# Earlier filler weights, a seventh key tile and later layer-two tables in a two-layer attention kernel

## The chip, the cores and the metric

The kernel runs on one NeuronCore of a Trainium2 chip. The metric is the device time of one execution in microseconds (us). Two executions of this kernel are told apart when they differ by more than about 0.2%, some 5 us.

## The reference

Two transformer layers over 2048 tokens of width 1024, in float32. Layer one projects x into queries, keys and values of six stick-breaking heads, six differential heads and four memory heads, and into gates; layer two has sliding-window attention with sinks in place of the first two. Each layer multiplies its mixed heads by silu(gate), applies an output matrix, adds the scaled input and normalises.

```python
log_1mb = where(strict, log_sigmoid(-z), 0);  after = reverse_cumsum(log_1mb) - log_1mb
sb_o    = where(strict, exp(log_sigmoid(z) + after), 0) @ v               # stick-breaking
df_o    = rms_norm((softmax(s[0]) - lam * softmax(s[1])) @ v, g) * 0.8    # differential
mem_o   = softmax(mq @ mk.T / 8) @ mv                                     # memory
y       = concat(sb_o, df_o, mem_o) * silu(gate) @ w_out
x       = layer_norm(sqrt(2) * x + y, g, b)        # sqrt(2) = (2 * DEPTH) ** 0.25
```

Queries and keys of the differential heads and of layer two are rotated (`_partial_rope`) by tables of cosines and sines.

## The kernel before

The program is one long sequence of stages, in each of which TensorE (PE) is given the most to do. Each f32 product of a projection is made of three matmuls on a high and a low part of its operands (hi·hi, hi·lo, lo·hi); `wtile`, `wsplit` and `split` make such parts with a cast on ScalarE (ACT) and a subtraction on GpSimd (POOL) or VectorE (DVE).

- `layer1_proj`, about 0 to 700 us: tiles of 128 output features by four token chunks of 512 (`t`), 24 matmuls each, into three PSUM banks ("mm"). Features 0 and 1 of its middle loop (`k` = 0, 1) are the memory queries. Beside each of their eight chunks `next(tables)` computes one step of the rotation tables: four steps of layer one (`rope1`), then four of layer two (`rope2`). A step is one DMA of positions, some eight DVE instructions, and on ACT an Abs and two Sin. From `k` = 2 a memory unit runs beside each chunk (`next(side)`): scores, softmax, transposes, values. The last part, `gates`, is 32 chunks of sigmoid and multiply.
- `stick_breaking`, about 715 to 1076 us: three pairs of heads `p`, each with four query chunks `t` = 3, 2, 1, 0, four blocks `qi` of 128 queries in each, and key chunks `c` = t to 0. A unit (p, t, qi, c) is scores on PE, two sigmoids on ACT, two scans on DVE, two multiplications on POOL, two groups of transposes on PE with copies on ACT and DVE, and value products on PE. Scores are made three units (`SB_AHEAD`) ahead of the transposes. Here SyncE (SP), PE, DVE and ACT run in the order of the code, and POOL in the order of a scheduler. `begin(p, t)` issues loads when the scores of a chunk begin.
- `differential`, about 1076 to 1616 us: three pairs, each in two halves `k` of four units `j`: scores, exponentials, a mixture of two softmaxes, transposes, values. Beside it `filler` makes part of the output projection from five of its eight weight tiles: it loads raw weights into three "rx" buffers (`wload`), splits them (`wsplit`: ACT cast, POOL subtraction), and works through 32 blocks. Its first steps, the ones before the first `yield`, run inside `stick_breaking`: four in `begin(2, 1)`, and one beside each of the last ten units. PE and ACT run in the order of the code here, the rest in the scheduler's.
- Keys of the differential stage are tiles of 512 keys, named "kc" (three buffers) and "kd" (three). `load_dk` picks the tag from a list by the number of the load; a load into a buffer waits until the tile before it there has been read. Pair 0 is loaded in `begin(2, 1)`. The next pair's chunks 3, 2 and 1 are asked for at the end of a pair's first half and chunk 0 at the end of its second. Values come through four "vc" buffers (`load_dv`).
- `join`, `layer2_kv`, `gates`, `layer2` and a last `out_proj` follow. In `out_proj` each block of 128 rows ends in a layer norm: mean and variance on DVE (`bn_aggr`), plus epsilon and power -0.5 on POOL, and a scaling on DVE.

All DMAs but a few are issued by SP, in one order. A DMA names the semaphores that it waits for, and those behind it wait with it.

Of the kernel before, what the change touches and what calls it, by code (L numbers as in the profile page):

```python
# [8 lines left out]
F32R = mybir.dt.float32r  # L9
# [8 lines left out]
P = 128  # L18
NB = S // P
TC = 512  # L20
NT = S // TC
NEG = -1e30
ALPHA = 4.0 ** 0.25
EPS = 1e-5
# [8 lines left out]
FT = 1  # L33
# [33 lines left out]
class Net:  # L67
# [216 lines left out]
    def layer1_proj(self):  # L284
        nc, dr = self.nc, self.dr
# [33 lines left out]
        for k, dst in enumerate((0, 1, self.sbq[1], self.sbk[1], self.sbq[2], self.sbk[2])):  # L319
            w = nxt  # L320
            for t in range(NT):
                ps = self.proj_t(w, t)
                if k < 2:
                    q = self.t("c2")
                    nc.scalar.mul(q, ps, 0.125)  # L325
                    for hh in range(2):
                        qs = self.t("c2", F32R)
                        self.qstack_head(qs, q, hh, nc.gpsimd)
                        self.dma(self.mq[dst, t, :, hh], qs)
                    next(tables)  # L330
                else:
                    self.spill_parts(ps, dst, t)
                    next(side)
                if t == 1:
                    nxt = self.wtile(W[rows[k + 1]]) if k < 5 else self.vtile(0)
                if t == 2 and k > 1 or t % 2 and k < 2 and k + t < 4:
                    next(kvs)
            if k == 1:
                side = self.memory(*self.mkv)
                kvs = self.memkv(self.i["wmo"], mem, False)  # L340
                next(kvs)
# [11 lines left out]
        for p in range(3):  # L353
            for base, dst in ((9, self.dfq), (12, self.dfk)):
                w = nxt
                for t in range(NT):
                    if t == 2:
# [8 lines left out]
        gates = self.gates(W[20:28], self.silu, self.om, self.m1,  # L366
                           [(f, t) for f in range(6) for t in range(NT)] + [(f, t) for t in range(NT) for f in (6, 7)])
        for k, _ in enumerate(gates):
            if k == 24 + GATES_A:
                qs = self.load_qstack(self.sbq[0], NT - 1)  # L370
                self.sb_first = (*self.load_sb(0), qs)
# [171 lines left out]
    def stick_breaking(self):  # L543
# [9 lines left out]
        def begin(p, t):  # L553
            sls[p, t] = self.load_silu(self.silu[p], t)
            k = chunks.index((p, t)) + 1
            if k < len(chunks):
                qs[chunks[k]] = self.load_qstack(self.sbq[chunks[k][0]], chunks[k][1])
            if t == NT - 2 and p < 2:
                kv[p + 1] = self.load_sb(p + 1)
            if p == 2 and t == FT:  # L560
                self.fill = self.filler()
                steps.extend(next(self.fill))
                for f in steps[:4]:
                    f()
                del steps[:4]
                self.dk, self.dq = {}, {}
                self.load_dq(0, 0, 0)
                for c in range(NT):
                    self.load_dk(0, c)
# [66 lines left out]
        for k, u in enumerate(units):  # L636
            if k + SB_AHEAD < len(units):
                scores(units[k + SB_AHEAD])
            turn(u)
            if k + SB_AHEAD < len(units):  # L640
                weights(units[k + SB_AHEAD])
            if u[0] == 2 and k > len(units) - 11:
                for f in steps[:1]:
                    f()
                del steps[:1]
            while k - done >= SB_GROUP or k == len(units) - 1 and done <= k:
                for v in units[done:done + SB_GROUP]:
                    values(v)
                done += SB_GROUP
        self.nc = nc  # L650

    def differential(self):
# [21 lines left out]
                f()  # L674
            del steps[:k]

        for c in range(NT):
            self.load_dv(0, c)
        for s in range(-2, len(units)):
            scores, new = self.diff_scores(units[s + 2], rows) if s + 2 < len(units) else ([[]] * 4, [])  # L680
# [30 lines left out]
        return [None] * (14 - len(tail)) + tail  # L711

    def load_dk(self, p, c):
        k_ = self.t(("kc", "kc", "kc", "kd", "kd", "kd", "kc", "kc", "kd", "kc", "kd", "kc")[len(self.dk)], F32R, [P, 4, 512])
        for g in range(4):
            self.dma(k_[32 * g:32 * g + 32], self.dfk[p][g // 2, :, c * 512:c * 512 + 512].rearrange("(h r) t -> r h t", h=4))
        self.dk[p, c] = k_
# [22 lines left out]
    def diff_scores(self, unit, rows):  # L740
# [15 lines left out]
        def chunk(hc, w, c):  # L756
            nc = self.nc
            qb, t, qi, n, col = parts[w]
            nch = (n + 511) // 512
            if c == 0 and w == 0:  # L760
                if hc == 0:
                    begin()
                rows[unit][0].append((self.t("row"), self.tiny(8, tag="mn", bufs=8)))
            e, mn = rows[unit][0][hc]
            mn = mn[:, 4 * w:4 * w + 4]
            lo, hi = c * 512, min(n, c * 512 + 512)
            m = hi - lo
            z = self.psum("z")
            diag = hi == n
            q = self.dq[p, k, j // 2, w][:, hc, (qi % 2) * P:(qi % 2 + 1) * P]  # L770
            nc.tensor.matmul(z[:, :m], q, self.dk[p, c][:, hc, :m], start=True, stop=True)
            before = mn[:, :1] if w and c else 3e38
            acc, n0 = mn[:, c:c + 1], max(0, m - 3 * P) if diag else m
            if n0:
                nc.vector.tensor_scalar(e[:, col + lo:col + lo + n0], z[:, :n0], -scale, before, ALU.mult, ALU.min, accum_out=acc)  # L775
            if diag:
                nc.vector.tensor_tensor_reduce(e[:, col + lo + n0:col + hi], z[:, n0:m], self.mask[:, 3 * P + n0 - m:3 * P], -scale,
                                               acc if n0 else before, ALU.add, ALU.min, acc)
            if w and c == 0:
                first, k_ = rows[unit][0][hc][1], (parts[0][3] + 511) // 512  # L780
                nc.vector.tensor_reduce(first[:, :1], first[:, :k_], AX.X, ALU.min)  # L781
            if diag and w and hc == 3 and j == 3 and p < 2:
                for c in ((3, 2, 1) if k == 0 else (0,)):
                    self.load_dk(p + 1, c)

        def exps(hc, w):
# [123 lines left out]
    def filler(self):  # L910
# [7 lines left out]
        def wload(h, k):  # L918
            raws[k] = self.t("rx", F32, [P, 512])
            self.dma(raws[k], i["woute"][tiles[k], :, 512 * h:512 * h + 512])  # L920
# [33 lines left out]
        def finish(f):  # L954
# [1 line left out]
            self.nc.vector.scalar_tensor_tensor(res[f], res[f], ALPHA, res["ps"], ALU.mult, ALU.add)  # L956
            self.dma(self.rp[tb, :, 512 * h:512 * h + 512], res[f])

        yield ([lambda: load(0)] + [lambda k=k: wload(0, k) for k in range(3)]
               + [f for k in range(5) for f in (lambda k=k: wsplit(0, k), *([lambda k=k: wload(0, k + 3)] if k < 2 else []))]  # L960
               + [lambda: split(0), lambda: load(1)])
        for f in range(len(blocks)):
            p = [lambda f=f, c=c: products(f, c) for c in range(5)]
            r, s, l, e = lambda f=f: resid(f), lambda f=f: split(f + 1), lambda f=f: load(f + 2), lambda f=f: finish(f)
# [63 lines left out]
    def out_proj(self, w, msrc, spans, res, alpha, lng, lnb, tbs, ahead):  # L1028
# [20 lines left out]
        for k, tb in enumerate(tbs):  # L1049
# [15 lines left out]
            mvr = self.tiny(2)  # L1065
            nc.vector.bn_aggr(mvr, st.rearrange("p (a s) -> p a s", a=2))
            rs = self.tiny(1)
            nc.gpsimd.tensor_scalar_add(rs, mvr[:, 1:2], EPS)  # L1068
            nc.gpsimd.tensor_tensor(rs, rs, self.mhalf[:, :1], ALU.pow)
            nc.vector.scalar_tensor_tensor(r, r, mvr[:, 0:1], g, ALU.subtract, ALU.mult)  # L1070
            if alpha:
# [344 lines left out]
    def run(self):  # L1416
        nc, dr, i = self.nc, self.dr, self.i
        with self.phase({"c2": 3, "sl": 2}, {}):
# [9 lines left out]
            self.rp = dr.tile([NB, P, D], F32, name="rp")  # L1428
            self.silu2 = [dr.tile([P, S], F32, name=f"silu2_{f}") for f in range(8)]
            self.m2 = dr.tile([8, P, S], F32, name="m2")  # L1430
            with self.phase({"qd": 2, "wT": 7, "vc": 4, "row": 9},
                            {"mm": 1, "z": 3, "tp": 2, "pv": 2}):
                tail = self.differential()
            keys.close()
# [88 lines left out]
```

## Time and profile before

| | |
|---|---|
| time, median of 3 runs | 2544.74 us (2543.16 to 2546.1) |
| the profiled execution | 2546.16 us, its span 2544.40 us |
| TensorE busy | 2392.6 us, 94% |
| VectorE, ScalarE, GpSimd busy | 62%, 49%, 37% |
| mean granted TensorE clock | 0.984 |

The profile is of one execution. The span is the time between its first and its last instruction. Busy time is counted per engine; for TensorE the ends of matmuls are modelled. "Idle before <-X" is the time in which an engine stood still before an instruction, with what released it. The granted clock is a share of 2.4 GHz; half of it is 1.2 GHz.

### The profile page before, as it was taken

Reading aid. Unit: us, or ns where it says so; the run is one execution under the profiler, and the core shown is the slowest. Engines: PE = TensorE matmul, PEld = TensorE weight load, DVE = VectorE, ACT = ScalarE, POOL = GpSimd, SP = SyncE. Lnnn points to the kernel's source line nnn. Section 1 sums busy time; section 2 is a strip of 40 time slices with the busy share of each in tenths; the row PEclk is TensorE's granted clock in tenths of the full one; section 3 lists DMA queues with packets and bytes.
Section 4 is the critical chain, followed back from the end, with each engine's and each line's share of the span. In section 5 each row is a group of like instructions: output and inputs, shape, how many; then the busy total and the mean of one; then the engine's idle time right before and its main releaser. Section 6 shows DMA issues by size and latency. Waiting matters only on the chain. (4 is left out here: it accounts for less than half of the span.)

```text
span 2544.4 us, 42300 instructions
## 1 busy us (share of the span) xinstructions
PE 2392.6 (94%) x15564; PEld 1939.8 (76%) x15564; DVE 1573.6 (62%) x3657; ACT 1254.2 (49%) x2453; POOL 939.3 (37%) x800
## 2 busy tenths in 40 slices
PE   9999999999999999789889888899999999999998
PEld 7778998888877777557667666778788777777887
DVE  5733222431168888699899899684312676777455
ACT  4443222221158777567677677443212777776100
POOL 0401002750057878611111021464612655534333
PEclk9999999999999999899999999999999999999999
DMA  7643222331334431944543341563323655533641
GB/s 280 208 156 131 82 84 79 127 132 56 107 90 111 93 84 34 215 122 109 128 112 94 103 109 46 181 204 109 86 98 112 163 153 154 144 97 101 199 144 64
DMA packets 199247, 311.60 MB, mean 122 GB/s; under 512 B 17920, under 2 KB 97280, under 8 KB 198528
## 3 DMA queue, kind: packets, MB, share of 16 engines
q1 hardware_dynamic: 198464, 307.83, 40.8%
q8 instruction: 124, 2.03, 0.4%
q10 hardware_dynamic: 576, 1.05, 0.1%
q14 instruction: 83, 0.68, 0.1%
HBM read 204.74 MB, written 104.07 MB: 121 GB/s over the span
## 5 line engine op out<-in xcount | busy, mean ns | idle before, releaser
L57 PE MATMUL psmm<-big,w 128*128 128x512 f32 x1680 | 414.9, 395 | 1.3 <-ACT c L325 1.3
L57 PEld LDWEIGHTS psmm<-big,w 128*128 128x128 f32 x1680 | 306.6, 189 | 59.4 <-ACT c L325 1.5
L57 ACT COPY wT<-pstp 128x512 f32<-128x512 f32 (+3 forms) x400 | 203.4, 525 | 188.6 <-PE pstp L57 185.0
L608 POOL TENSOR_TENSOR wb<-wb,row 128x512 f32<-128x512 f32 (+3 forms) x240 | 262.6, 1117 | 72.8 <-DVE row L57 47.5
L57 DVE TENSOR_TENSOR_SCAN row<-s,row,pszero 128x512 f32<-128x512 f32 (+5 forms) x240 | 254.3, 1105 | 51.8 <-ACT s L57 33.4
L254 PE MATMUL psmm<-big,w 128*128 128x512 f32 x1200 | 275.2, 390 | 0.0
L254 PEld LDWEIGHTS psmm<-big,w 128*128 128x128 f32 x1200 | 225.1, 188 | 46.9 <-issue 0.2
L57 PE MATMUL psmm<-big,mp 128*128 128x512 f32 x1056 | 246.6, 394 | 3.4 <-POOL big L1015 3.4
L57 ACT ACTIVATE row<-row,mn 128x2048 f32<-128x2048 f32 (+7 forms) x192 | 229.8, 1202 | 13.9 <-DVE mn L781 10.1
L57 PEld LDWEIGHTS psmm<-big,mp 128*128 128x128 f32 x1056 | 199.7, 190 | 45.3 <-POOL big L1015 3.8
L775 DVE TENSOR_SCALAR_CACHE_REDUCE row<-psz 128x512 f32<-128x512 f32 (+1 forms) x324 | 200.2, 640 | 20.7 <-PE psz L57 19.8
L1234 DVE TENSOR_TENSOR c<-psmm,c 128x512 f32<-128x512 f32 x62 | 42.7, 691 | 240.3 <-ACT c L1233 240.3
L945 POOL TENSOR_TENSOR mp<-mp,mp 128x640 fp32r<-128x640 f32 x32 | 52.0, 1625 | 343.4 <-ACT mp L57 282.7
L57 PE MATMUL pstp<-ident,wb 128*128 128x128 f32 x816 | 118.2, 277 | 35.4 <-DVE wT L57 15.4
L817 DVE SCALAR_TENSOR_TENSOR row<-row,tiny,row 128x128 f32<-128x128 f32 (+7 forms) x144 | 149.4, 1088 | 0.4
L57 PE MATMUL psmm<-wo,mp 128*128 128x512 f32 x480 | 147.7, 420 | 1.4 <-POOL mp L945 0.9
L209 POOL TENSOR_TENSOR w<-w,w 128x1024 fp32r<-128x1024 f32 x20 | 48.8, 2440 | 256.3 <-ACT w L208 107.5
L1233 ACT ACTIVATE c<-psmm 128x512 f32<-128x512 f32 x62 | 36.8, 596 | 212.8 <-PE psmm L254 204.5
L57 PE MATMUL pstp<-ident,row 128*128 128x128 f32 x816 | 130.5, 281 | 6.4 <-ACT wT L57 5.6
L57 PEld LDWEIGHTS pstp<-ident,wb 128*128 128x128 f32 x816 | 92.2, 141 | 56.6 <-POOL wb L608 24.8
L1191 ACT ACTIVATE e<-e,tiny 128x256 f32<-128x256 f32 (+1 forms) x192 | 94.7, 494 | 60.5 <-DVE e L1189 60.1
L57 PEld LDWEIGHTS pstp<-ident,row 128*128 128x128 f32 x816 | 99.6, 143 | 30.8 <-ACT wT L57 13.4
(232 smaller groups left out, 5003.0 us busy)
## 6 DMA issues: line engine op xcount, KB each, us to landing
silu<-c SPq DMA_DIRECT2D x54, 256.0 KB, 2.3
sl<-silu SPq DMA_DIRECT2D x54, 256.0 KB, 3.3
qs<-sbq SPq DMA_DIRECT2D x48, 256.0 KB, 5.3
cs<-rope SPq DMA_DIRECT2D x24, 512.0 KB, 4.6
kc<-k SPq DMA_DIRECT2D x36, 320.0 KB, 5.0
w<-in_we_dram SPq DMA_DIRECT2D x20, 512.0 KB, 3.6
raw<-in_wo_dram SPq DMA_DIRECT2D x20, 512.0 KB, 3.8
rx<-in_x_dram SPq DMA_DIRECT2D x32, 256.0 KB, 2.7
```

The source lines that it names most:

```text
L57: return self.tc.keep_in_program_order(f(*a, **k))
L209: eng.tensor_sub(lo[:, sl], raw[:, sl], hi[:, sl].bitcast(F32))
L254: self.nc.tensor.matmul(ps, w[a][:, c, :], self.xpart(t, c, b), start=(c == k == 0), stop=(c == 7 and k == 2))
L608: nc.gpsimd.tensor_mul(w[:, hh, :m], w[:, hh, :m], prr[:, lo:hi])
L775: nc.vector.tensor_scalar(e[:, col + lo:col + lo + n0], z[:, :n0], -scale, before, ALU.mult, ALU.min, accum_out=acc)
L817: self.nc.vector.scalar_tensor_tensor(x[:, lo:hi], y[:, lo:hi], cf[hh][:, w:w + 1], x[:, lo:hi], ALU.mult, ALU.add)
L945: self.nc.gpsimd.tensor_sub(ml, m, mh.bitcast(F32))
L1191: nc.scalar.activation(e[:, hh, ns:], e[:, hh, ns:], AF.Exp, bias=nmx[:, hh:hh + 1], scale=-1.0, accum_out=s[:, hh:hh + 1])
L1233: nc.scalar.activation(sg, ps, AF.Sigmoid)
L1234: nc.vector.tensor_mul(sg, ps, sg)
```

## The change

- The four `rope2` steps move from the chunks of `k` = 1 to the gates, ahead of chunks 2, 7, 12 and 17.
- The filler's first steps begin in `begin(2, 3)`: three weight loads there, the five splits and the other two loads beside the units of chunk (2, 3) with odd `c`. The loads and the split of the first two mixed blocks run beside chunk (2, 1). The differential stage's first queries and keys are asked for in `begin(2, 2)`.
- A seventh key tile "ke" exists during `differential`; the list of tags is new, and all four chunks of the next pair are asked for at the end of a pair's first half. The first values are loaded in the order 3, 0, 1, 2.
- In `out_proj` epsilon is added on DVE in place of POOL.

```diff
@@ layer1_proj
-                    next(tables)
+                    if k == 0:
+                        next(tables)
...
         for k, _ in enumerate(gates):
+            if k % 5 == 2 and k < 20:
+                next(tables)
@@ stick_breaking, begin
-            if p == 2 and t == FT:
+            if p == 2 and t == NT - 1:
                 self.fill = self.filler()
                 steps.extend(next(self.fill))
-                for f in steps[:4]:
+                for f in steps[:3]:
                     f()
-                del steps[:4]
+                del steps[:3]
+            if p == 2 and t == NT - 2:
                 self.dk, self.dq = {}, {}
@@ stick_breaking, loop over units
-            if u[0] == 2 and k > len(units) - 11:
-                for f in steps[:1]:
-                    f()
-                del steps[:1]
+            if steps and (u[0] == 2 and u[1] == NT - 1 and u[3] % 2 and len(steps) > 3 or u[0] == 2 and u[1] == FT):
+                steps.pop(0)()
@@ differential
-        for c in range(NT):
+        for c in (3, 0, 1, 2):
             self.load_dv(0, c)
@@ load_dk
-        k_ = self.t(("kc", "kc", "kc", "kd", "kd", "kd", "kc", "kc", "kd", "kc", "kd", "kc")[len(self.dk)], F32R, [P, 4, 512])
+        k_ = self.t(("kc", "kc", "kc", "kd", "kd", "kd", "ke", "kd", "kc", "kc", "kc", "kd")[len(self.dk)], F32R, [P, 4, 512])
@@ diff_scores
-            if diag and w and hc == 3 and j == 3 and p < 2:
-                for c in ((3, 2, 1) if k == 0 else (0,)):
+            if diag and w and hc == 3 and j == 3 and k == 0 and p < 2:
+                for c in range(NT - 1, -1, -1):
@@ filler
-        yield ([lambda: load(0)] + [lambda k=k: wload(0, k) for k in range(3)]
+        yield ([lambda k=k: wload(0, k) for k in range(3)]
...
-               + [lambda: split(0), lambda: load(1)])
+               + [lambda: load(0), lambda: load(1), lambda: split(0)])
@@ out_proj
-            nc.gpsimd.tensor_scalar_add(rs, mvr[:, 1:2], EPS)
+            nc.vector.tensor_scalar_add(rs, mvr[:, 1:2], EPS)
@@ run
-            with self.phase({"qd": 2, "wT": 7, "vc": 4, "row": 9},
+            with self.phase({"qd": 2, "wT": 7, "vc": 4, "row": 9, "ke": 1},
```

DVE, first memory unit, before. Lines 181 to 188 are a table step; L486, L491 and L495 are the softmax (maximum, reciprocal, scaling) of the scores `psz`:

```order
L182 TENSOR_SCALAR c_159_1015<-c_159_1015,freq 128x512
L184 TENSOR_SCALAR c_160_1018<-c_159_1015 128x512
L185 TENSOR_SCALAR c_160_1018<-c_160_1018 128x512
L187 SCALAR_TENSOR_TENSOR c_159_1015<-c_160_1018,c_159_1015 128x512
L486 TENSOR_REDUCE tiny_1072<-psz_1066 128x2
L265 TENSOR_TENSOR c_165_1059<-psmm_1033,c_164_1058 128x512
L187 SCALAR_TENSOR_TENSOR c_159_1015<-c_160_1018,c_159_1015 128x512
L491 RECIPROCAL tiny_1077<-tiny_1074 128x2
L187 SCALAR_TENSOR_TENSOR c_159_1015<-c_160_1018,c_159_1015 128x512
L495 TENSOR_SCALAR c_168_1071<-c_168_1071,tiny_1077 128x256 x2
```

The same place in the change (the softmax's lines are three higher):

```order
L469 COPY mv_263<-psmm_872 128x128
L469 COPY mv_263<-psmm_882 128x128
L489 TENSOR_REDUCE tiny_1004<-psz_998 128x2
L265 TENSOR_TENSOR c_153_991<-psmm_965,c_152_990 128x512
L494 RECIPROCAL tiny_1009<-tiny_1006 128x2
L498 TENSOR_SCALAR c_156_1003<-c_156_1003,tiny_1009 128x256 x2
```

No table step stands ahead of the softmax or inside it any more.

SP in the third pair of `stick_breaking`, before. `rx<-in_woute` are raw weights, `qs` the queries and `sl` the gates of a chunk, `m<-c` a chunk's result, `qa`, `kc` and `kd` the first queries and keys of the next stage:

```order
L57 DMA rx_9765<-in_woute_dram 128x512
L57 DMA rx_9767<-in_woute_dram 128x512
L57 DMA rx_9769<-in_woute_dram 128x512
L57 DMA qa_9771<-dfq_241 32x4x256 x4
L57 DMA qa_9776<-dfq_241 32x4x256 x4
L57 DMA kc_9781<-dfk_244 32x4x512 x4
L57 DMA kc_9786<-dfk_244 32x4x512 x4
L57 DMA kc_9791<-dfk_244 32x4x512 x4
L57 DMA kd_9796<-dfk_244 32x4x512 x4
L57 DMA m_255<-c_1761_9941 128x512
L113 DMA kd_11131<-dfk_245 32x4x512 x4
L113 DMA kd_11136<-dfk_245 32x4x512 x4
L57 DMA rx_10055<-in_woute_dram 128x512
```

And in the change, two chunks earlier in the stage:

```order
L57 DMA qs_8766<-sbq_237 64x2x512 x4
L57 DMA rx_8771<-in_woute_dram 128x512
L57 DMA rx_8773<-in_woute_dram 128x512
L57 DMA rx_8775<-in_woute_dram 128x512
L57 DMA m_255<-c_1533_8903 128x512
L57 DMA rx_8966<-in_woute_dram 128x512
L57 DMA rx_9116<-in_woute_dram 128x512
L57 DMA sl_9343<-silu_251 128x512
L113 DMA rx_10382<-in_x_dram 128x512
L57 DMA qs_9345<-sbq_237 64x2x512 x4
L57 DMA qa_9350<-dfq_241 32x4x256 x4
```

Before, the fourth weight load stands behind 24 loads of keys; in the change all five stand ahead of them, and of the queries of chunk (2, 1).

## Rows read from the trace of the kernel before

**Rows 1.** The page's first part: busy us, share of the span and instructions of PE and the other engines.

```profile
PE 2392.6 (94%) x15564; PEld 1939.8 (76%) x15564; DVE 1573.6 (62%) x3657; ACT 1254.2 (49%) x2453; POOL 939.3 (37%) x800
```

**Rows 2.** Stretches of the span: from and to, length, busy us (and instructions) of PE, weight loads, DVE, ACT and POOL, then the granted clock, the DMA share and GB/s.

```profile
100.00:200.00 100.00, 91.23 (x468) 74.37 (x469) 47.87 (x93) 41.99 (x91) 15.38 (x9) 0.95 0.50 162
...
600.00:700.00 100.00, 100.00 (x443) 82.86 (x442) 15.77 (x23) 11.38 (x19) 0.00 (x0) 1.00 0.28 88
...
1000.00:1100.00 100.00, 77.34 (x629) 60.84 (x627) 70.05 (x127) 58.52 (x93) 56.20 (x72) 0.90 0.74 175
```

**Rows 3.** What PE waited for, over the whole span: us in total, times, the longest.

```profile
PE psz L57 <- DVE row L775: 31.9, 51, 2.5
PE pstp L57 <- ACT wT L57: 21.5, 16, 14.1
...
PE psz L57 <- DMA kc<-dfk: 8.4, 2, 6.9
PE pstp L57 <- DVE c L495: 7.8, 1, 7.8
```

**Rows 4.** PE in order of time at the first memory units: start, us, instruction, count, idle time before it. `psz` are scores, `pstp` transposes, `psmm` the 24 matmuls of a projection.

```profile
117.50 0.64 PE L57 MATMUL psz<-w,w 128*128 128x256 f32 x4
...
131.37 1.11 PE L57 MATMUL pstp<-ident,c 128*128 128x128 f32 x4 [7.77 <-DVE c L495]
...
133.13 6.90 PE L57 MATMUL psmm<-big,w 128*128 128x512 f32 x24
...
158.25 0.66 PE L57 MATMUL pstp<-ident,c 128*128 128x128 f32 x4
...
166.34 5.63 PE L57 MATMUL psmm<-big,w 128*128 128x512 f32 x24
```

**Rows 5.** DVE and ACT there, in order of time: the first and the last DVE instruction of a table step, the maximum of the first scores, and ACT's table load ahead of their exponentials.

```profile
116.16 2.64 DVE L181 CAST c<-c 128x512 f32<-128x512 int32 x1 [5.92 <-DMA c<-in_pos_dram]
...
124.33 0.43 DVE L188 TENSOR_SCALAR c<-c 128x512 f32<-128x512 f32 x1
...
127.19 0.68 DVE L486 TENSOR_REDUCE tiny<-psz 128x2 f32<-128x512 f32 x1
...
127.95 1.28 ACT L489 ACT_TABLE_LOAD   x1 [0.78 <-DVE tiny L486]
```

**Rows 6.** SP's issues in the third pair, and one cast and one subtraction of a filler weight on ACT and POOL. The us of an SP row run from its first issue to the end of its last.

```profile
945.06 2.53 SPq L57 DMA_DIRECT2D qs<-sbq  x4
...
983.86 2.53 SPq L57 DMA_DIRECT2D qs<-sbq  x4
...
1018.34 3.59 SPq L57 DMA_DIRECT2D qs<-sbq  x4
...
1024.66 5.80 SPq L57 DMA_DIRECT2D qa<-dfq  x8
...
1048.27 8.82 SPq L113 DMA_DIRECT2D kd<-dfk  x8
1057.96 0.35 SPq L57 DMA_DIRECT2D rx<-in_woute_dram  x1
...
1067.02 0.62 ACT L57 CAST wo<-rx 128x512 fp32r<-128x512 f32 x1 [15.34 <-DMA rx<-in_woute_dram]
...
1067.72 1.27 POOL L925 TENSOR_TENSOR wo<-rx,wo 128x512 fp32r<-128x512 f32 x1 [12.88 <-ACT wo L57]
```

**Rows 7.** PE at the end of the stick-breaking stage; the last row is the first product of the differential stage.

```profile
1041.73 1.75 PE L57 MATMUL pspv<-wT,kv 128*64 128x128 f32 x28
...
1052.88 1.31 PE L57 MATMUL pspv<-wT,kv 128*64 128x128 f32 x20
1068.27 0.87 PE L57 MATMUL pstp<-ident,wb 128*128 128x128 f32 x3 [14.08 <-ACT wT L57]
...
1071.98 2.96 PE L57 MATMUL pspv<-wT,kv 128*64 128x128 f32 x28
...
1076.05 0.96 PE L57 MATMUL psz<-kc,qa 128*128 128x512 f32 x3
```

**Rows 8.** Two stretches of that pair, columns as in Rows 2: chunk (2, 3), and the units beside which three of the weights were split.

```profile
945.00:984.00 39.00, 36.59 (x344) 29.68 (x342) 35.19 (x38) 31.53 (x47) 31.02 (x34) 1.00 0.24 55
...
1040.00:1054.00 14.00, 12.73 (x134) 10.57 (x132) 10.14 (x13) 10.61 (x19) 13.39 (x18) 1.00 1.06 214
```

**Rows 9.** PE and DVE where the second and the third pair of the differential stage begin.

```profile
1250.38 1.19 PE L57 MATMUL psz<-kc,qa 128*128 128x512 f32 x2 [6.85 <-DMA kc<-dfk]
...
1251.18 0.69 DVE L775 TENSOR_SCALAR_CACHE_REDUCE row<-psz 128x512 f32<-128x512 f32 x1 [4.20 <-PE psz L57]
...
1422.76 0.47 PE L57 MATMUL psz<-kc,qa 128*128 128x512 f32 x1 [1.55 <-DMA kc<-dfk]
...
1423.26 0.69 DVE L775 TENSOR_SCALAR_CACHE_REDUCE row<-psz 128x512 f32<-128x512 f32 x1 [1.66 <-PE psz L57]
```

**Rows 10.** DVE and POOL in the last layer norm: variance, subtraction of the mean, epsilon, power.

```profile
2537.73 0.21 DVE L1066 BATCH_NORM_AGGREGATE tiny<-st 128x2 f32<-128x12 f32 x1
2537.98 1.28 DVE L1070 SCALAR_TENSOR_TENSOR rx<-rx,tiny,gb 128x1024 f32<-128x1024 f32 x1
...
2538.03 1.31 POOL L1068 TENSOR_SCALAR tiny<-tiny 128x1 f32<-128x1 f32 x1 [8.91 <-DVE tiny L1066]
2539.43 0.57 POOL L1069 TENSOR_TENSOR tiny<-tiny,mhalf 128x1 f32<-128x1 f32 x1
```

## The prediction

> **What bounds the kernel now.** I read the page's busy shares first. TensorE (PE) is busy 94% of the span [rows 1], so what a change of order can win is at most the 6% in which PE stands still, some 150 us, plus matmuls at the lower clock after a stop. The stretches come next: PE is full in the gates (600 to 700 us), 91.23 us of 100 busy from 100 to 200, and 77.34 of 100 from 1000 to 1100, where the granted clock falls to 0.90 [rows 2]. The list of PE's waits then sorts the idle time [rows 3]. Two kinds are there. Many short waits for DVE (51 times, 31.9 us in all) are the differential stage running at DVE's pace, and nothing in the change makes that DVE work smaller. A few long ones are single events: 14.1 us for a copy on ACT, 7.8 us for a softmax, 8.4 us in two waits for keys. The change touches all three, so I price each at its place, in order of time.
>
> **1. Rotation tables out of the memory queries.** The first memory scores end at 117.50 + 0.64 = 118.14 us, and the transposes of their softmax start at 131.37 after 7.77 us of idle, so PE was there at 123.60 [rows 4]. DVE took up the maximum only at 127.19, because a whole table step (116.16 to 124.76) and half of the next stood ahead of it; from the maximum to the transposes 4.2 us pass, a table load of 1.28 on ACT among them [rows 4, 5]. The order of the change has no step there. The softmax then starts near 118.2 and is done near 122.4, 1.2 us before PE comes, so the wait goes whole: 7.8 us. After the stop PE ran for a while at the lower of its two clock levels, 1.2 GHz: the four transposes took 1.11 in place of 0.66 and the 24 matmuls 6.90 in place of 5.63 [rows 4], 1.7 more. I take -9.5, with -5 as the weak end, should the softmax start 3 us later than I think.
>
> The four steps return in the gates, where PE has no idle time and ACT is 11% busy [rows 2]. Their cover is this: a chunk keeps PE 5.63 us [rows 4], and with three PSUM banks a sigmoid may be two chunks late, 11.3 us. At worst ACT waits for a whole step on DVE (8.6 us from 116.16 to 124.76) and then does its own part, two table loads at 1.28 and three instructions of some 0.62 (a cast's time), 4.4: 13.0 in all, 1.7 beyond the cover, 6.9 for four [rows 5, 6]. I take 0, since DVE is idle in most of that stage, and keep 0 to +6.9.
>
> **2. Filler weights ahead of the keys.** On the path at the end of stick-breaking stands ACT: its queue holds a cast of the fourth weight, the cast waits 15.34 us for a load, and a copy that PE needs is queued behind the cast. SP had issued that load only at 1057.96, after queries and keys from 1024.66 to 1057.09, and it took until 1067.02 [rows 6]. PE shows the other side: last products end at 1054.19, then 14.08 idle, then a tail with 28 value products in 2.96 us in place of 1.75, and the next stage begins at 1076.05 [rows 7]. That is 21.86 us. The tail lasts 7.78 of them, from 1068.27. If all of it shrinks as 2.96 does to 1.75 it takes 4.6, so the most that can go is 17.3, and the least, with the tail as slow as now, 14.1. In the change no weight is split in the tail, which also frees POOL of two subtractions of 1.27 there [rows 6]. What is late next is the chain of the last units through ACT, DVE and POOL; I leave 0.8 us for it and take -16.5.
>
> The weights now cost time in chunk (2, 3). POOL is busy 31.02 of 39 us there and gets 5 x 1.27 = 6.4 more; ACT gets 5 x 0.62 = 3.1 on 31.53 [rows 6, 8]. Both fit, but each split stands between two multiplications that PE waits for. If none is absorbed, that is 5 x 1.89 = 9.5 us; if all are, 0. The nearest row is the stretch with three such splits: PE busy 12.73 of 14, 91%, beside 94% without any [rows 8]. Three points of 39 us are 1.2; I take twice that, +2.5, since POOL has less room here.
>
> SP's queue must not become late. The first three loads are issued behind the queries of 945.06, so at 947.6; casts come three units later, and a unit lasts (983.86 - 945.06) / 16 = 2.43 us [rows 6], so about 952.3. A load that takes the 9.06 us of the one at 1057.96 would hold ACT 4 us, which the 9.5 covers. The keys are asked for behind the queries of 983.86; if the 32.4 us from 1024.66 to 1057.09 are shifted to 986.4 they end at 1018.8, when the next queries' buffer comes free anyway (1018.34) [rows 6]. Cost 0.
>
> **3. Key tiles.** The first products of the second pair wait 6.85 us for keys and those of the third 1.55 [rows 9]. Their loads went into buffers that the pair before still read. With "ke" and the new list every chunk goes to a buffer that has been read by the end of a half pair. But the stage runs at DVE's pace, so what counts is DVE's idle time behind these waits: 4.20 and 1.66 [rows 9]. I take -5.9. The ends are 0, if other waits fill the place, and -8.4, if PE's whole wait comes back. The order of the first values' loads changes nothing that PE waits for.
>
> **4. Epsilon on DVE.** In the last layer norm POOL's addition takes 1.31 us, from 2538.03 to 2539.34, and the power 0.57 behind it; DVE's subtraction beside them runs from 2537.98 to 2539.26 [rows 10]. So POOL's time is DVE's time: it was held until DVE ended. On DVE the addition costs up to 0.21, like the variance [rows 10]; the power then lies beside the subtraction instead. If it is held likewise it ends after it by up to 0.57; if not, the subtraction's end decides. That is -0.5 to 0; I take -0.3.
>
> The Trainium skill, "SBUF — State Buffer", on the shared port pair, says that DVE and GpSimd lock each other out of it for whole instructions, the loser blocking fully. By that rule the trace agrees, 1.31 beside 1.28. Taken without the rule, the edit would look like 1.31 - 0.21 = 1.1 us.
>
> **Sum.** -9.5 - 16.5 + 2.5 - 5.9 - 0.3 = -29.7. The profiled execution took 2546.16 (span 2544.40 and 1.76 around it), so 2516.5 by its measure; it lies 1.4 above the median of 2544.74, so I predict 2515.
>
> **Rivals.**
> - *POOL holds chunk (2, 3).* For it: POOL would be busy 37.4 of 39 us [rows 8]. Against it: it still fits, and three units of lead absorb some. Price 9.5 in place of 2.5, and the 5.9 of the keys lost to DVE's pace as well at worst: 2522 to 2528.
> - *The keys' waits only change their name.* DVE waits in the differential stage are the commonest row [rows 3]. Then term 3 is 0 and the time 2521.
> - *The tail shrinks by more, and PE's whole key waits come back.* 17.3, 8.4 and no cost in chunk (2, 3): 2509.
> - *ACT's queue blocks on the weights in their new place, slower than before.* Its place is chunk (2, 3): each of the first, fourth and fifth casts waits for a load that SP reaches late, since the fourth and fifth loads wait in SP's queue for POOL to free a buffer. The price is that of the one such event in the trace, 15.34 us each [rows 6]. Two eat the gain of 29.7 and give about 2546, no change; three give 2561. The point from which it decides is a lead of cast over load below 9.06 us. Against it: the late loads have four units of lead or more, 9.7 us.
>
> The instruction order of PE shows that the change does what it says, so that is no rival.
>
> **Chances.** Forecast 0.62; POOL 0.13; keys 0.10; the larger gain 0.10; ACT blocked 0.05, of which slower 0.03 and no change 0.02. The forecast's own range is 2509 to 2522. The range that should hold 8 in 10 takes in the first rivals: 2506 to 2527. Faster or slower means by over 0.2%, 5 us, about what a measurement of this kernel can tell: faster 0.95, same 0.02, slower 0.03.
>
> **What would show it.** The profile of the change should have no PE wait for DVE L495's counterpart near 123 us; no wait of PE over 3 us between 1040 and 1070, and the differential stage beginning some 24 us earlier than 1076 (9.5 of it from step 1, less 2.5); no PE wait for a DMA of keys. Wrong signs would be ACT waiting for `rx<-in_woute` in chunk (2, 3), PE waiting for POOL there by more than 5 us, PE idle in the gates, or short DVE waits in the differential stage growing by the 6 us that the keys give.

## The result, and the profile after

The changed kernel took 2525.86 us (median of 6 runs) beside 2545.5 of the kernel before; the ratio is 0.9931, with an interval of 0.9919 to 0.9943. That is 19.6 us gained where 29.7 were forecast. Later, beside other kernels, it took 2527.69 us against 2544.57 (0.9936, 0.9921 to 0.9950). On the 2544.74 us that the prediction started from, the ratio gives 2527.2, just above the range of 2506 to 2527.

When PE starts each stage shows where the gain came and where it stopped (us from the start of the span, in the profiled executions; "again" is the second profile of the changed kernel):

| kernel | stick-breaking, first scores | differential, first scores | `join`, first product | differential stage |
|---|---|---|---|---|
| before | 719.7 | 1076.0 | 1616.4 | 540.4 |
| changed | 708.0 | 1050.5 | 1596.0 | 545.5 |
| changed, again | 708.4 | 1049.5 | 1591.6 | 542.1 |

Up to the differential stage 25.5 us are won (23.5 forecast). The stage then grows by 5.1 and 1.7 us where it was to shrink by 5.9. From the first product of `join` to the end both kernels take nearly the same, 928.0 us before and 928.5.

What PE waited for, over the span of the changed kernel: us in total, times, the longest.

```profile
PE psz L57 <- DVE row L777: 33.5, 53, 3.1
PE psz L57 <- DVE mn L779: 17.0, 18, 2.1
...
PE pstp L57 <- ACT wT L57: 10.0, 16, 1.9
PE pstp L57 <- POOL rx L1078: 6.0, 4, 3.1
...
PE psmm L57 <- ACT mp L57: 5.5, 1, 5.5
```

Beside [rows 3] the waits of 14.1, 7.8 and 8.4 us are gone. A single wait of 5.5 for a block of the filler is new (it ends at 1069.44 us; the prediction had no wait over 3 us there), and the longest wait for a DVE reduction is 3.1 in place of 2.5. The two groups of short waits for DVE grow from 46.4 to 50.5 us together: one of the wrong signs that the prediction named, in part. The waits for POOL's `rx`, nearly all in the layer norms of `join`, were 2.9.

Stretches, columns as in [rows 2]:

```profile
100.00:200.00 100.00, 100.00 (x543) 82.30 (x543) 30.04 (x72) 32.89 (x81) 14.93 (x9) 1.00 0.41 140
600.00:700.00 100.00, 100.00 (x443) 82.84 (x442) 25.46 (x41) 19.68 (x29) 0.10 (x1) 1.00 0.43 126
1000.00:1100.00 100.00, 83.28 (x611) 63.42 (x607) 82.63 (x178) 61.04 (x99) 48.37 (x61) 0.95 0.66 156
```

PE is full where the tables stood and stays full where they went. PE at the first memory units, as in [rows 4]:

```profile
115.93 0.64 PE L57 MATMUL psz<-w,w 128*128 128x256 f32 x4
...
121.88 0.60 PE L57 MATMUL pstp<-ident,c 128*128 128x128 f32 x4
```

The transposes come 5.3 us after the scores end, with no wait. The end of the stick-breaking stage, as in [rows 7], has lost its 14.08:

```profile
1043.46 1.06 PE L57 MATMUL pstp<-ident,wb 128*128 128x128 f32 x8 [1.26 <-POOL wb L612]
...
1047.63 1.75 PE L57 MATMUL pspv<-wT,kv 128*64 128x128 f32 x28
...
1050.50 0.97 PE L57 MATMUL psz<-kc,qa 128*128 128x512 f32 x3
```

At the start of the differential stage the trace shows what no step of the prediction had priced. SP's issues in order of time, then ACT:

```profile
1048.08 1.81 SPq L113 DMA_DIRECT2D ke<-dfk  x4
1049.99 4.46 SPq L113 DMA_DIRECT2D vc<-v  x4
1055.28 7.84 SPq L113 DMA_DIRECT2D qd<-dfq  x8
1063.43 0.97 SPq L113 DMA_DIRECT2D mp<-m  x2
```

```profile
1056.64 0.19 ACT L57 ACTIVATION_READ_ACCUMULATOR row<-row,mn 128x1 f32 x1
1068.66 0.72 ACT L57 CAST mp<-mp 128x640 fp32r<-128x640 f32 x1 [11.83 <-DMA mp<-m]
1069.29 2.00 ACT L57 ACTIVATE row<-row,mn 128x2048 f32<-128x2048 f32 x1
```

The seventh tile's buffer is free from the start of the stage, so the scheduler wrote its loads first in SP's queue, though its keys are read only by the second pair, 180 us later. Values, queries and the filler's third block stand behind them. ACT runs in program order; its cast of that block waits 11.83 us, and the exponentials behind the cast wait with it. Before, the same wait was 6.40:

```profile
1088.77 0.72 ACT L57 CAST mp<-mp 128x640 fp32r<-128x640 f32 x1 [6.40 <-DMA mp<-m]
```

Where the second pair begins, PE's wait for keys is gone too, but DVE and PE read:

```profile
1215.45 0.68 DVE L777 TENSOR_SCALAR_CACHE_REDUCE row<-psz 128x512 f32<-128x512 f32 x1
...
1216.06 3.79 DVE L819 SCALAR_TENSOR_TENSOR row<-row,tiny,row 128x1024 f32<-128x1024 f32 x3
1219.78 0.68 DVE L777 TENSOR_SCALAR_CACHE_REDUCE row<-psz 128x512 f32<-128x512 f32 x1
```

```profile
1220.52 0.49 PE L57 MATMUL psz<-kc,qd 128*128 128x512 f32 x1 [3.13 <-DVE row L777]
1220.94 3.11 PE L57 MATMUL pspv<-wT,vc 128*64 128x128 f32 x32
```

Three mixes now stand ahead of a reduction that PE needs; in the kernel before that reduction stood ahead of them:

```profile
1235.57 0.68 DVE L775 TENSOR_SCALAR_CACHE_REDUCE row<-psz 128x512 f32<-128x512 f32 x1
...
1236.17 0.68 DVE L775 TENSOR_SCALAR_CACHE_REDUCE row<-psz 128x512 f32<-128x512 f32 x1
...
1236.79 3.09 DVE L817 SCALAR_TENSOR_TENSOR row<-row,tiny,row 128x1024 f32<-128x1024 f32 x3
```

```profile
1237.66 1.97 PE L57 MATMUL pspv<-wT,vc 128*64 128x128 f32 x32
```

In the changed kernel PE waits 3.13 us, then makes 32 value products in 3.11 in place of 1.97, in part at the lower clock of 1.2 GHz (the granted clock was 0.64 of 2.4 GHz from 1220.6 to 1224).

### The profile page after: what moved, and what is told of

Its sections match the earlier page's. It is cut to its first block, busy times and chain, and to the rows that moved or that the text cites. A ratio compares the mean times of both kernels' runs of the same rounds, so it can differ in the third digit from the quotient of the medians.

```text
span 2524.5 us, 42315 instructions
## 1 busy us (share of the span) xinstructions
PE 2390.9 (95%) x15564; PEld 1939.1 (77%) x15564; DVE 1572.5 (62%) x3689; ACT 1262.1 (50%) x2459; POOL 939.6 (37%) x768
```

## The experiments

Theory A: SP's queue at the stage's start costs 5.4 us. Theory B: the order in which DVE's instructions are written eats what the keys give. Rival C: a wait for keys is worth nothing, since DVE's pace fills it. D (the filler's move itself makes the third block late) and E (what is won at one place is given back at the next stop) came up on the way. A profile shows a cause at its place. The times alone tell less: of the changed kernel's variants only "order, loads on ACT" and "two ahead" have ratios whose intervals lie below its own.

A yardstick for all of them: ACT runs 192 exponentials in this stage, always in one order. This is by how many us a given one starts later than in the kernel before, both counted from the stage's first scores. The 57th and 67th lie on either side of the second pair's start, the 93rd and 95th around unit (1, 0, 3), the 137th in the third pair. The last columns are the stage and the median time.

| kernel | 3rd | 57th | 67th | 93rd | 95th | 137th | 185th | stage | time |
|---|---|---|---|---|---|---|---|---|---|
| changed | 5.4 | 5.5 | 6.4 | 5.3 | 5.9 | 3.0 | 4.9 | 545.5 | 2525.9 |
| changed, again | 5.5 | 5.7 | 5.2 | 4.3 | 4.6 | 3.0 | 1.5 | 542.1 | 2527.7 |
| keys alone | 4.9 | 6.1 | 4.4 | 3.4 | 3.1 | 1.7 | 3.4 | 544.1 | 2547.2 |
| filler alone | 1.1 | 1.6 | 0.8 | -1.7 | 3.7 | 5.2 | 5.2 | 545.7 | 2535.0 |
| tables alone | -1.1 | 0.0 | 0.3 | 0.3 | 0.8 | -2.5 | -0.5 | 540.1 | 2534.3 |
| loads on ACT | -0.3 | 3.0 | 5.7 | 4.7 | 5.0 | 1.9 | 0.3 | 540.9 | 2524.7 |
| order | 5.9 | 4.9 | -0.6 | -3.3 | 1.8 | -1.2 | 0.4 | 541.1 | 2523.2 |
| order, loads on ACT | -0.3 | 2.4 | -0.8 | -3.3 | 1.6 | -1.5 | 0.1 | 540.7 | 2520.4 |
| no keys | -0.4 | 1.5 | 2.5 | 1.2 | 1.9 | -0.8 | 0.9 | 541.5 | 2523.3 |
| filler, order | -0.7 | 3.2 | 5.2 | 4.7 | 4.5 | 6.4 | 4.8 | 545.5 | 2535.3 |
| two ahead | -0.5 | 2.9 | -0.5 | -1.3 | -2.4 | -3.4 | -1.7 | 538.9 | 2517.9 |
| DVE pinned | 0.0 | -3.8 | -10.6 | -6.2 | -7.0 | -1.3 | 6.5 | 548.0 | 2527.2 |

**Keys alone**: of the diff, only the hunks on `load_dk`, `diff_scores`, the first values and "ke".

> The kernel before with the key part alone (seventh tile, new list of buffers, all four loads of the next pair at the end of a half pair, new order of the first values). Theory A (queue: the seventh tile's four loads stand in SP's queue ahead of values, queries and the filler's third block, and a cast on ACT waits for that block) expects ACT's longest wait for mp<-m at the stage's start to grow from 6.4 to about 11.8 us, +5.4. Theory B (order: where the second pair begins, the changed kernel has one reduction of DVE written behind three mixes, which eats what the keys give, and that order comes with the filler's move, not with the keys) expects the second pair's join to gain 4 us here, since DVE's order there is that of before, and the third pair's 3. Both together: differential stage 540.4 + 5.4 - 4.2 - 2.9 = 538.7 us, time about 2544. Rival C (pace: a key wait is worth nothing, DVE's pace fills it whatever the order) expects the stage at 540.4 + 5.4 = 545.8 and 2551 us.

Measured: 2547.18 us, ratio 1.0006 (0.9996 to 1.0015): no gain at all. The cast waits 11.26 us and the third exponential starts 4.9 late, as A says. At the second pair 1.7 come back, not 4.2: more than C allows and less than B asks, and the time lies between the two. DVE's order there is that of before, two reductions ahead of the mixes, but at PE's next stop, 2.14 us for DVE, 28 value products behind it take 2.92 us in place of 1.75.

**Filler alone**: only the hunks of `stick_breaking` and of the filler's first list.

> The kernel before with the filler's weights alone at their new place. All theories expect the stick-breaking stage 13.85 us shorter, as in the changed kernel. Theory B expects DVE's changed order where the second pair begins, hidden there at least in part by the wait of 6.85 us for keys, which is still there: differential stage 540 to 543 us, time 2531.5 to 2534.5. Theory A expects no ACT wait for mp<-m above about 6.4 us at the stage's start, since no seventh tile is loaded there. Rival D (the filler's move itself makes the third block late, because the first two blocks are loaded earlier and the stage starts with less in hand) expects that wait at about 10 us and the stage near 545.

Measured: 2534.98 (0.9958, 0.9943 to 0.9972). Stick-breaking shrinks by 16.1 to 340.3. D falls: the cast waits 7.51 us and the third exponential is 1.1 late, no more. At the second pair one reduction has moved behind the mixes, as in the changed kernel; PE waits 3.06 us there for DVE and no longer for keys, though no seventh tile exists. But the stage grows to 545.7, 5.4 of it between the 93rd and the 95th exponential, where again a reduction had moved behind three mixes. That order alone does not make the 5.4: in the changed kernel the same reduction stands behind the mixes too, and the step is 0.6 and 0.3. There PE waits 1.48 us and makes the next 32 value products in 1.97; here it waits 2.70 and makes them in 3.68, with a granted clock of 0.54 in that stretch.

**Tables alone**: only `next(tables)` under `k == 0` and among the gates.

> The kernel before with the layer-two tables alone among the gates. Theory of the prediction: the stick-breaking stage begins 9.5 us earlier by the prediction's sum, 11.7 by the trace of the changed kernel, and nothing else moves: 2533.8 us, with the differential stage at 540.4 us. Rival: the gain shrinks later, since DVE's order in the differential stage changes with it too: stage 541 to 545.

Measured: 2534.30 (0.9961, 0.9946 to 0.9976), stage 540.1; in this profile stick-breaking begins 8.9 us earlier. The first theory holds.

**Loads on ACT**:

```diff
         for g in range(4):
-            self.dma(k_[32 * g:32 * g + 32], self.dfk[p]...)
+            self.dma(k_[32 * g:32 * g + 32], self.dfk[p]..., self.nc.scalar if len(self.dk) == 6 else None)
```

> The changed kernel with the seventh tile's four loads issued from ACT's queue, in program order at the end of the first half pair, not from SP's. Theory A expects ACT's wait for mp<-m at the stage's start to fall from 11.8 to between 6.4 and 10 us (the four issues took 1.81 us of SP, the values behind them took 1.2 longer than before), the differential stage at 540 to 543.6 us and the time at 2520.5 to 2524, less some 1.4 us of issuing on ACT where its queue is not full. The rival D (the third block is late whatever stands ahead of it) expects no change, 2525.9.

Measured: 2524.71 (0.9924, 0.9909 to 0.9938), stage 540.9. The cast, without the tile's loads in SP's queue:

```profile
1065.28 0.73 ACT L57 CAST mp<-mp 128x640 fp32r<-128x640 f32 x1 [6.14 <-DMA mp<-m]
```

6.14 in place of 11.83: A is shown for the stage's start. Only 1.8 us of it is the issue of the tile's four loads; behind them the issue of the values took 4.46 us in place of 2.80, and the block itself took 5.2 us from its issue to the cast in place of 4.2. But little of the 5.7 can be seen later. At the 57th exponential 2.5 are left: 1.8 go early, and 1.3 at the 35th, where a cast waits 1.23 us for another block. At the 67th 0.7 is left beside the changed kernel's first profile and nothing beside its second (5.7 and 5.2). Of that, 1.5 is a step at the 59th that the changed kernel doesn't have: 24 products take 2.52 us in place of 1.53, at the lower clock. The time is above the expected 2520.5 to 2524 and not told apart from the changed kernel's.

**Order** (the changed kernel), with an edge in the scheduler's graph that carries no semaphore:

```diff
+FIRST = (((0, 1, 3), 3, 0, 1), ((1, 0, 3), 3, 0, 0))
...
+                if (unit, hc, w, c) in FIRST:
+                    self.first = red
...
+                    if hh == 0 and unit in [f[0] for f in FIRST]:
+                        self.tc.add_manual_dep(ins.ins, self.first.ins.name, ...NoSync...)
```

Each entry of `FIRST` names a unit and one of its reductions; the mixes of that unit's first pair of rows are put behind that reduction.

> The changed kernel with DVE's order at two places as before: one reduction again ahead of the three mixes of unit (0, 1, 3), where the second pair begins, and one ahead of those of (1, 0, 3). Theory B (the order that the filler's move brought eats what the keys give) expects the PE wait of 3.1 us at the second pair's join to go and the stage to shrink from 545.5 to 540.5 to 542.5 us, time 2521 to 2523. Rival C (pace: key waits are worth nothing here) expects the waits to take another name once more, stage 545 to 546, time 2525.9.

Measured: 2523.17 (0.9915, 0.9894 to 0.9935), stage 541.1. DVE and PE at the second pair, to be held against the rows of the changed kernel above (lines are one to three further down):

```profile
1213.56 0.68 DVE L778 TENSOR_SCALAR_CACHE_REDUCE row<-psz 128x512 f32<-128x512 f32 x1
...
1214.17 3.19 DVE L822 SCALAR_TENSOR_TENSOR row<-row,tiny,row 128x1024 f32<-128x1024 f32 x3
```

```profile
1214.73 0.40 PE L58 MATMUL psz<-kc,qd 128*128 128x512 f32 x1
1215.06 1.97 PE L58 MATMUL pspv<-wT,vc 128*64 128x128 f32 x32
```

PE doesn't wait, and from the 57th to the 67th exponential 5.5 us are won where the changed kernel loses 0.9 (its second profile wins 0.5). B is shown at its place, and C falls there. Then 5.1 are given back between the 93rd and the 95th:

```profile
1298.23 2.73 DVE L822 SCALAR_TENSOR_TENSOR row<-row,tiny,row 128x512 f32<-128x512 f32 x3
...
1307.33 0.69 DVE L778 TENSOR_SCALAR_CACHE_REDUCE row<-psz 128x512 f32<-128x512 f32 x1 [3.91 <-PE psz L58]
```

```profile
1301.62 0.80 PE L58 MATMUL psz<-kd,qd 128*128 128x512 f32 x1 [2.18 <-DVE row L778]
1302.35 3.68 PE L58 MATMUL pspv<-wT,vc 128*64 128x128 f32 x32
```

PE, earlier now, waits 2.18 us for a reduction behind the mixes, falls to its lower clock (granted 0.50 from 1301.6 to 1306.5) and holds up DVE for 3.91.

**Order, loads on ACT**: both edits.

> Both repairs: the seventh tile's loads on ACT's queue and the two reductions ahead of the mixes. Theories A and B together expect the stage, 540.9 us with the first repair alone, at 536 to 538.5 us, and the time at 2519.5 to 2522. Rival C expects 540.9 and 2524.7.

Measured: 2520.39 (0.9900, 0.9883 to 0.9918), stage 540.7. The start and the second pair are both won, and at unit (1, 0, 3) 4.9 go. The time is in the range, the stage is not: the two gains don't add up to the end. At the 67th exponential this kernel stands at -0.8 and "order", which starts 6.2 us later, at -0.6: here, too, almost nothing of the late start is left.

**No keys**: the changed kernel with the hunks of "keys alone" undone.

> The changed kernel without the key part and with the first values in their old order: tables, filler and epsilon alone. If the key part costs as a whole (A and B), this is no slower than the changed kernel: tables 11.7 and filler 11.0 from 2546.0 give 2523.3 us, the stage at 542.5 to 545.7, with no ACT wait for mp<-m over 6.4 at its start. If the key part is worth its 5.9 and something else was lost, it is slower than the changed kernel, 2531.8.

Measured: 2523.32 (0.9913, 0.9892 to 0.9934), stage 541.5. As a whole the key part gave nothing: with it the changed kernel took 2525.9 and 2527.7. Its 5.9 us are refuted as a net gain. The second pair's start shows why:

```profile
1216.62 0.50 PE L57 MATMUL psz<-kc,qd 128*128 128x512 f32 x1 [3.15 <-DVE row L777]
1217.05 3.15 PE L57 MATMUL pspv<-wT,vc 128*64 128x128 f32 x32
```

Without the seventh tile PE has the same wait for DVE as in the changed kernel, and none for keys. The filler's move had already put a wait for DVE where the wait for keys was, so the tile had nothing left to win there.

**Filler, order**: the filler's move alone, with the edges of "order".

> The kernel before with the filler's move alone and the same two reductions ahead of the mixes. Theory B expects the step of 5.4 us that the filler alone shows at unit (1, 0, 3) to go: stage 545.7 to 540 to 541.5 us, time 2530 to 2531.5. Rival: that step is not DVE's order but POOL or a late load, and stays: 545.7 and 2535.

Measured: 2535.27 (0.9957, 0.9940 to 0.9974), stage 545.5. The step at unit (1, 0, 3) goes, as B says (4.7 to 4.5), but the stage is no shorter: PE waits 5.15 us for keys at the second pair instead, so the 67th exponential is 5.2 late and not 0.8. B's forecast of the stage is wrong here. Without the tile the right order brings the wait for keys back; with the tile and the wrong order the wait is DVE's. Each repair needs the other.

**Two ahead**: "order, loads on ACT", with one more reduction ahead of the mixes of unit (1, 0, 3).

```diff
-FIRST = (((0, 1, 3), 3, 0, 1), ((1, 0, 3), 3, 0, 0))
+FIRST = (((0, 1, 3), 3, 0, 1), ((1, 0, 3), 3, 0, 1))
```

> Both repairs of the run before, and at unit (1, 0, 3) two reductions ahead of the three mixes in place of one. Theory E (what the repairs win is given back there: PE, now earlier, stops 2.2 us for a reduction behind the mixes and then runs 3.7 us of value products at its lower clock) expects that step of 5.1 us to shrink by 3 to 5: stage 535.5 to 538 us, time 2515 to 2518. Rival C (pace: the stage comes to 541 whatever the order) expects the gain back under another name, 540 to 541 and 2520.4.

Measured: 2517.94 (0.9899, 0.9886 to 0.9912), stage 538.9. The same place:

```profile
1303.93 0.69 DVE L779 TENSOR_SCALAR_CACHE_REDUCE row<-psz 128x512 f32<-128x512 f32 x1 [0.70 <-PE psz L58]
...
1304.55 2.74 DVE L823 SCALAR_TENSOR_TENSOR row<-row,tiny,row 128x512 f32<-128x512 f32 x3
```

```profile
1305.10 0.39 PE L58 MATMUL psz<-kd,qd 128*128 128x512 f32 x1
1305.42 1.97 PE L58 MATMUL pspv<-wT,vc 128*64 128x128 f32 x32
```

No wait, 1.97 us for the products, and the step of 4.9 is a gain of 1.1. E holds at its place. For the whole it isn't shown: the stage is 0.9 over its expected range and 1.8 under that of "order, loads on ACT", and the ratios of the two, 0.9899 and 0.9900, are the same. This kernel has the lowest median of the study, 9.8 us under the changed kernel beside it.

**Changed, again**: the changed kernel, not edited.

> The changed kernel once more beside the others, for their difference on one chip: 2524 to 2527 us, the stage at 545.5 if a kernel's stage is the same in each execution, and the wait of 11.8 us for mp<-m at its start in its place again.

Measured: 2527.69 us, stage 542.1, and the wait at its start is there again (11.94). The start and the second pair repeat within 0.5 us up to the 65th exponential; from there the stage loses 3.4 less, so a stage is known to some 3 us from one profile.

**DVE pinned**: "loads on ACT", with `PinnedCore(..., ("tensor", "scalar", "vector"))` in `differential`.

> The seventh tile's loads on ACT's queue, and all of DVE's instructions of the differential stage in the order in which the program is written, not in the scheduler's. Theory B expects an effect of order well over 1 us. The written order puts four reductions of the next unit ahead of nearly every pair of mixes, so PE waits less for reductions and ACT longer for mixed rows: between 532 us (if PE's waits for DVE, 33 us in all, shrink by a fourth) and 560 (if the transposes wait for mixes). Rival C (pace): 541 again, whatever the order.

Measured: 2527.16 (0.9931, 0.9912 to 0.9950), stage 548.0. By the 67th exponential 10.6 us are won and by the 185th 17.1 lost again. Order is worth far more than the key waits; a fixed 541 is refuted. Behind the stage this kernel takes 923.5 us where the changed one takes 928.5, so the stage's length alone is not its price.

## Why the prediction was right and wrong

- **Step 1, tables, -9.5: right.** Stick-breaking begins at 709.2 us in the mean of the nine profiles with the tables moved and at 719.9 in the four without: -10.7. The gates hid the steps (PE 100.00 of 100).
- **Step 2, filler weights, -16.5 + 2.5: right in its place.** The stick-breaking stage lasts 341.4 us in the mean of ten profiles with the move and 356.5 in the three without: -15.1 for -14.0. Within it chunk (2, 3) lost 0.9 to 4.2 us, 2.1 in the mean (2.5 forecast), and what follows won 17.2 (16.5 forecast). POOL did not hold that chunk (0.5 us of PE's waits around it are for POOL), and ACT waited for a weight there once, 2.36 us, so neither rival came true. What the step left out is that the move also changes DVE's order in the next stage. With the filler alone that stage is 545.7 for 540.4; one step of it goes with the order, but not the sum ("filler, order"), so this growth is not settled.
- **Step 3, key tiles, -5.9: this step failed.** The stage that it was to shorten measured +5.1 and +1.7, so 9.3 us off in the mean, about the whole miss; beside "no keys", where the stage is 541.5, the key part itself measured +4.0 and +0.6. The working said "what counts is DVE's idle time behind these waits", read in the kernel before, and looked neither at what step 2 does to DVE's order nor at any other queue. In place of the gain stood this. At the second pair the wait did change its name, as the rival had it, but not because of DVE's pace: with the filler's move three mixes stand ahead of one reduction, and PE waits 3.13 us for DVE with the tile and 3.15 without it ("no keys"). With the tile and that order repaired 5.5 us are won there; the changed kernel lost 0.9, or won 0.5 in its second profile, so the order cost 5.0 to 6.4 (shown by "order"). The tile's own loads, issued 180 us early ahead of a load that ACT waits for in order, cost the start 5.7 us (shown by "loads on ACT"), but what of that reaches the stage's end is not shown: the changed kernel is 4.0 us behind "no keys" at the 57th exponential and 4.0 and 0.6 at the end, while with the loads on ACT, or with the order repaired, the start's part was gone by the 67th. And what is won at one place was partly lost at the next stop of PE (shown by "order" and "two ahead"). Of 8.4 us of waits [rows 9], 3.2 to 5.5 could be had at the second pair once the order was right. The 3 us of the third pair come without the key part as well ("no keys", "tables alone") and are not its own. What the stage gains or loses behind the second pair is known to some 3 us only, and its sum stays open.
- **The sentence "The order of the first values' loads changes nothing that PE waits for"** was not tried apart from the tile.
- **Step 4, epsilon, -0.3: right in its place, nothing in the sum.** In the last norm, as in [rows 10]:

```profile
2517.82 0.21 DVE L1068 BATCH_NORM_AGGREGATE tiny<-st 128x2 f32<-128x12 f32 x1
2518.07 0.15 DVE L1070 TENSOR_SCALAR tiny<-tiny 128x1 f32<-128x1 f32 x1
2518.14 1.27 DVE L1072 SCALAR_TENSOR_TENSOR rx<-rx,tiny,gb 128x1024 f32<-128x1024 f32 x1
2519.86 1.42 DVE L1075 SCALAR_TENSOR_TENSOR rx<-rx,tiny,gb 128x512 f32<-128x512 f32 x2 [0.44 <-POOL tiny L1071]
```

```profile
2518.30 1.52 POOL L1071 TENSOR_TENSOR tiny<-tiny,mhalf 128x1 f32<-128x1 f32 x1 [9.36 <-DVE tiny L1070]
```

  In the kernel before the scaling came here:

```profile
2540.03 1.41 DVE L1073 SCALAR_TENSOR_TENSOR rx<-rx,tiny,gb 128x512 f32<-128x512 f32 x2 [0.77 <-POOL tiny L1069]
```

  From the variance to the last scaling it is 2.04 us, and was 2.30 (2537.73 to 2540.03). Now it is the power that is held: it ends 0.41 us after DVE's subtraction and takes 1.52 in place of 0.57. The Trainium skill, "SBUF — State Buffer", section "Who interferes with whom", says that a DVE instruction with two inputs in SBUF contends with a GpSimd instruction that reads SBUF; this subtraction has two, and the trace agrees. The step looked at the last norm alone. The same code runs in `join`, and there PE's waits for POOL's `rx` are 6.0 us in place of 2.9, the longest 3.1 in all eight kernels with epsilon on DVE and at most 2.1 in the five without. No run has the epsilon edit by itself, so its price there is not shown; from `join` to the end the changed kernel takes 0.5 us more, not 0.3 less.

## What to carry to other kernels

When a buffer is added, ask when its load can be issued and what stands behind it in that queue: a load that is ready early is not free at its place if an engine in program order waits for the next one, even where, as here, little of the loss can be seen later. Where a scheduler writes one engine's order, an edit elsewhere can move a single instruction and cost as much as the wait it removes, so compare the written order at every place that a term rests on, and ask whether one part of a change has already replaced the wait that another part is to remove. In a stage where two engines wait for each other by turns, count a removed wait at its full size only up to the next stop.

## What was not expected of the hardware

The same stop can bring the lower clock in one execution and not in the next. PE in the changed kernel, in its first profile and in its second, at one place:

```profile
1452.06 1.00 PE L57 MATMUL psz<-kc,qd 128*128 128x512 f32 x2 [1.47 <-DVE mn L779]
...
1454.65 1.06 PE L57 MATMUL pstp<-ident,row 128*128 128x128 f32 x4
...
1455.93 1.40 PE L57 MATMUL psmm<-wo,mp 128*128 128x512 f32 x3
```

```profile
1451.09 1.00 PE L57 MATMUL psz<-kc,qd 128*128 128x512 f32 x2 [1.47 <-DVE mn L779]
...
1453.23 0.60 PE L57 MATMUL pstp<-ident,row 128*128 128x128 f32 x4
...
1453.90 0.86 PE L57 MATMUL psmm<-wo,mp 128*128 128x512 f32 x3
```

After the same wait of 1.47 us four transposes take 1.06 or 0.60 and three products 1.40 or 0.86. The granted clock was 0.61 from 1454 to 1458 us of the first and 1.00 from 1452.9 to 1457 of the second. The exponential behind them starts 1.6 us later for it. With the tables alone the third pair's 3 us are of this kind in part: behind one wait of 2.14 us there, four transposes and three products took 1.04 and 1.48 in the kernel before, 0.60 and 0.86 in that one. In the changed kernel the lower clock came there too (1.06 and 1.49). Why the clock falls in the one and not in the other stays open.
